# Eight PSUM accumulator tiles of one bank in place of two of four, in a decoder trunk on one core

## The chip, the core and the metric

The kernel runs on one core of one Trainium2 chip. The metric is the device time of one execution in microseconds (us), taken as the median of several runs. A profile is one further execution under the hardware profiler. The engines are named as in the profile: PE is TensorE's matmuls, PEld its weight loads, DVE is VectorE, ACT is ScalarE, SP issues the DMAs. L361 is line 361 of the kernel before.

## What is computed

Two layers over one sequence of 256 tokens and 2048 channels, in float32: a recurrent layer and an attention layer, each followed by a gated FFN with 5632 hidden channels.

```python
x = recurrent_block(x, norm1_g[0], lru_w_in, conv, gates, lru_lambda, lru_w_out)
x = swiglu_ffn(x, norm2_g[0], ffn_w_in[0], ffn_w_out[0])
k, v = shared_kv(x, kv_norm_g, w_kv, k_norm_g)
x = attn_block(x, norm1_g[1], w_q, q_norm_g, sinks, w_o, k, v)   # 32 heads of 64, window 128
x = swiglu_ffn(x, norm2_g[1], ffn_w_in[1], ffn_w_out[1])
...
def swiglu_ffn(x, g, w_in, w_out):
    gate, up = jnp.split(rms_norm(x, g) @ w_in, 2, axis=-1)
    return x + (jax.nn.silu(gate) * up) @ w_out
```

## The kernel before

**Jobs.** The work is a list of jobs, one for each weight tile of 128 x 1024 numbers (512 KB). `stream` (L335) goes through it: it loads the tile four jobs ahead, splits it three jobs ahead, and then issues the job's matmuls. A split (L306) makes of a float32 tile a rounded part `hi` on ScalarE (L314) and the rest `lo` on VectorE (L315). There are four buffers of each, so a split waits until PE has used the tile four jobs before. A product of two float32 matrices is three matmuls of such parts: hi by hi, hi by lo, and lo by hi.

**Groups.** Jobs come in groups that add up in four banks of PSUM (`group`, L365). A bank holds 512 float32 columns per partition, and there are eight. When the last job of a group is issued, `done` issues the operations that read its banks: `pull` (L398) or `residual` (L479, which adds into the residual stream `x`). The last job goes through the banks one after the other (L383), the earlier ones mix them. In some jobs (`SYNC`) a matmul is 512 columns wide and leaves two halves in a bank; then ScalarE copies one half to a temporary `t`, and VectorE adds the other.

**Banks.** `banks` is a queue of the eight banks: `bank` (L218) takes the first, `free_bank` puts one back at the end once its readers are issued, and `bank4` (L221) takes the four of one half of PSUM together, where all four are free. So a group has the four banks that were not in use by the group before it. Small products (norm statistics, transposes, scores, probabilities times values) take single banks with `mbank` (L240). In the kernel before, PSUM is two tiles, `b0` and `b1`, of four banks each, and a bank is a slice of one.

**Stages.** First the recurrent layer (`lru`): groups for four parts of the x branch and four of the y branch, and between them eight short gate jobs (`gates`, L839: 24 matmuls at L850 into four banks, each read by a sigmoid at L856), in the order x0 x1 x2 g0 x3 g1 y0 g2 g3 y1 g4 g5 y2 g6 g7 y3; then four groups of the output projection. Next an FFN with 22 groups into the hidden width and 4 out of it. Then keys and values, queries (L1235, two banks a group) with attention woven between, the output projection of attention (four groups), and the second FFN.

**Attention.** For each of 16 pairs of heads, `head_pair` issues: scores on PE (L1086), a masked sum and maximum on VectorE (L1097, which leaves the maximum in `h`), exponentials on ScalarE (L121), the division by their sum on VectorE (L139), transposes on PE (L1131), copies of these to SBUF on ScalarE (L121), the product with the values on PE (L1150), and a split of the result. The queries come to it through `finish`: splits of the query banks and transposes on PE (L1209).

**The product groups.** Groups 5, 7, ..., 17 of each FFN (`FAST`, seven per FFN) save matmuls: in six of their eight jobs seven products of 128 x 128 by 128 x 256 blocks stand for eight (`fast`, L541), and in the other two all eight are made (`plain`, L519). They add up in eight places of 256 columns, place h in bank h // 2 (`put`, L513). `joined` (L690) then sums the places into the gate and the up part, `at(h)` being place h. `fast` jobs write all places; the last job is `plain` and writes places 0 to 3 only, that is the two lower banks. A later job of the next group issues the transposes of the result (`turn`, L710, matmuls at L714).

**Order.** Each engine takes its instructions in order. The order in which the Python code issues them is set by half ticks of the job list (`half_tick`, `run_bg`), which let background tasks run as far as a count of VectorE and ScalarE time allows. The framework that builds the program then places each engine's instructions anew by what they depend on, and puts in the waits. All operations that go through `a`, `tt`, `stt`, `ts` have the lines L121, L130, L134, L139/L141.

## Time and profile before

| | us |
|---|---|
| median of 3 runs | 2086.24 (2085.16 to 2087.63) |
| profiled execution | 2089.25 |
| its span | 2087.5 |
| PE busy | 2013.3 (96%) |
| DVE busy | 1458.2 (70%) |
| ACT busy | 1125.1 (54%) |
| mean granted clock of PE | 0.989 |

The span is the time from the first to the last instruction of the profiled execution; the execution's own time lies a little above it. Busy times are shares of that span. A row of waits names who waited, for whose result, the time in total, how often, and the longest. In a row of the timeline the brackets at the end say how long the engine was idle before, and what ended that. PEclk is the clock that PE was granted, as a share of full speed.

### The profile page before, as it was taken

The numbers are of one execution on the slowest core, as the hardware profiler recorded it, in microseconds if no ns is written. First come the engines' busy times: TensorE is split into PE (matmuls) and PEld (weight loads), VectorE is DVE, ScalarE is ACT, GpSimd is POOL, SyncE is SP. The second block draws the span as 40 slices with busy tenths as digits, with TensorE's granted clock in tenths as the row PEclk, the third lists the DMA queues.
The fourth block names the chain that finished last, engine by engine and source line by source line (L and its number), as shares of the span: only waits on it lengthen the run. The fifth ranks groups of instructions, "written<-read, shape, count | busy, mean of one in ns | idle before, by whom it ended". The sixth has DMA issues, their size and how long they took to land. (4 is left out here: it accounts for less than half of the span.)

```text
span 2087.5 us, 39923 instructions
## 1 busy us (share of the span) xinstructions
PE 2013.3 (96%) x16487; PEld 1955.6 (94%) x16487; DVE 1458.2 (70%) x2291; ACT 1125.1 (54%) x1629; POOL 0.2 (0%) x4
## 2 busy tenths in 40 slices
PE   9999999999999999999998777999999999999999
PEld 9998999999999999999976567999999999999999
DVE  8878767888888955555576555677888889544443
ACT  7678755555555644444456555455555556444332
POOL 0000000000000000000000000000000000000000
PEclk9999999999999999999999999999999999999999
DMA  7545555555566655655652222545655565656663
GB/s 256 173 150 182 172 172 194 197 196 198 190 199 205 193 197 195 195 194 185 202 166 97 91 81 77 181 167 192 202 193 195 196 207 190 201 193 204 204 205 125
DMA packets 105016, 376.56 MB, mean 180 GB/s; under 512 B 11649, under 2 KB 13825, under 8 KB 104833
## 3 DMA queue, kind: packets, MB, share of 16 engines
q1 hardware_dynamic: 104544, 373.60, 54.1%
q8 instruction: 129, 2.11, 0.4%
q10 hardware_dynamic: 288, 0.40, 0.1%
q14 instruction: 55, 0.44, 0.1%
HBM read 371.86 MB, written 2.10 MB: 179 GB/s over the span
## 5 line engine op out<-in xcount | busy, mean ns | idle before, releaser
L361 PE MATMUL b<-s,hi 128*128 128x256 f32 (+1 forms) x8455 | 1138.6, 282 | 22.2 <-ACT s L121 8.5
L361 PEld LDWEIGHTS b<-s,hi 128*128 128x128 f32 x8455 | 1059.4, 189 | 38.2 <-ACT s L121 13.2
L315 DVE TENSOR_TENSOR lo<-raw,hi 128x1024 fp32r<-128x1024 f32 (+1 forms) x621 | 755.0, 1220 | 466.2 <-ACT hi L314 463.3
L314 ACT ACTIVATE hi<-raw 128x1024 fp32r<-128x1024 f32 (+1 forms) x621 | 653.4, 1056 | 636.0 <-PE b L361 497.9
L361 PE MATMUL b<-s,lo 128*128 128x256 f32 x4352 | 652.3, 278 | 0.9 <-DVE h L1097 0.9
L361 PEld LDWEIGHTS b<-s,lo 128*128 128x128 f32 x4352 | 568.9, 189 | 1.3 <-DVE h L1097 1.1
L328 ACT ACTIVATE s<-s 128x1024 fp32r<-128x1024 f32 x84 | 89.2, 1062 | 144.4 <-DVE s L327 143.6
L515 PE MATMUL b<-hi,s 128*128 128x256 f32 (+1 forms) x868 | 162.9, 291 | 0.0
L515 PEld LDWEIGHTS b<-hi,s 128*128 128x128 f32 x868 | 130.4, 189 | 3.8
L515 PE MATMUL b<-s,s 128*128 128x256 f32 x1008 | 133.3, 281 | 0.0
L515 PEld LDWEIGHTS b<-s,s 128*128 128x128 f32 x1008 | 125.2, 189 | 0.0
L330 DVE TENSOR_TENSOR s<-s,s 128x1024 fp32r<-128x1024 f32 x84 | 102.6, 1222 | 23.0 <-ACT s L328 22.3
L515 PE MATMUL b<-lo,s 128*128 128x256 f32 (+1 forms) x434 | 114.1, 289 | 0.0
L1235 PE MATMUL b<-hi,s 128*128 128x512 f32 x256 | 88.6, 427 | 14.3 <-ACT s L121 8.4
L121 ACT ACTIVATE s<-s 128x512 fp32r<-128x512 f32 (+3 forms) x172 | 82.9, 519 | 34.5 <-DVE s L130 25.1
L130 DVE TENSOR_TENSOR s<-s,s 128x512 fp32r<-128x512 f32 (+2 forms) x143 | 74.4, 549 | 12.1 <-ACT s L121 12.1
L121 ACT ACTIVATE s<-b 128x384 f32<-128x384 f32 (+4 forms) x112 | 51.1, 481 | 57.7 <-PE b L1235 10.8
L329 DVE TENSOR_TENSOR lo<-raw,hi 128x768 fp32r<-128x768 f32 x84 | 79.3, 950 | 0.0
L515 PEld LDWEIGHTS b<-lo,s 128*128 128x128 f32 x434 | 76.4, 188 | 1.8
L324 ACT ACTIVATE hi<-raw 128x768 fp32r<-128x768 f32 x84 | 70.2, 840 | 10.3 <-ACT hi L324 3.1
L1235 PEld LDWEIGHTS b<-hi,s 128*128 128x128 f32 x256 | 47.9, 199 | 27.7 <-ACT s L121 12.2
L325 DVE TENSOR_TENSOR s<-raw 128x512 f32<-128x512 f32 x84 | 57.6, 686 | 10.7 <-DMA raw<-in_ffn_in 10.6
(117 smaller groups left out, 1112.8 us busy)
## 6 DMA issues: line engine op xcount, KB each, us to landing
raw<-in_ffn_in SPq DMA_DIRECT2D x352, 512.0 KB, 3.4
raw<-in_ffn_out SPq DMA_DIRECT2D x176, 512.0 KB, 4.1
raw<-in_lru_in SPq DMA_DIRECT2D x63, 512.0 KB, 3.4
raw<-in_lru_out SPq DMA_DIRECT2D x32, 512.0 KB, 3.3
raw<-in_w_q SPq DMA_DIRECT2D x32, 512.0 KB, 3.3
raw<-in_w_o SPq DMA_DIRECT2D x32, 512.0 KB, 3.3
raw<-in_gate SPq DMA_DIRECT2D x8, 512.0 KB, 3.8
raw<-in_kv SPq DMA_DIRECT2D x8, 512.0 KB, 4.2
```

The costliest lines, as they stand in the source:

```text
L121: self.nc.scalar.activation(out, in_, func, **kw)
L130: self.nc.vector.tensor_tensor(out, a, b, op)
L314: self.nc.scalar.activation(hi[:, q], raw[:, q], AF.Copy)
L315: self.nc.vector.tensor_tensor(lo[:, q], raw[:, q], hi[:, q].bitcast(F32), ALU.subtract)
L324: act(hi[:, q], raw[:, q], AF.Copy)
L325: tt(two(d[:, 0:2 * T]), two(raw[:, T:3 * T]), raw[:, 0:T].unsqueeze(1).to_broadcast([P, 2, T]), ALU.subtract)
L328: act(mh[:, :], d[:, :], AF.Copy)
L329: tt(lo[:, q], raw[:, q], hi[:, q].bitcast(F32), ALU.subtract)
L330: tt(ml[:, :], d[:, :], mh[:, :].bitcast(F32), ALU.subtract)
L361: self.nc.tensor.matmul(ps[f][:, 0:c1 - c0], w, x2[k][:, c0:c1], start=f not in begun, stop=last and all(q[1] != f for q in todo[n + 1:]))
L515: nc.tensor.matmul(st["ps"][0][:, h * T:(h + n) * T], x, w, start=b not in st["begun"], stop=True, skip_group_check=True)
L1235: nc.tensor.matmul(st[g][b][:, :], x, q, start=c + kt == 0 and x is xh and q is wh, stop=c == 7 and kt == 1 and q is wl)
```

## The change

PSUM becomes eight tiles of one bank, `b0` to `b7`. The queue of banks, `bank4` and every matmul's place are as before: each matmul writes the same columns of the same physical bank. Since an instruction that reads two banks would now read two tiles, `joined` reads each with a sum of its own: the sum over places 3 and 4 and that over places 1 and 2 become two sums each, and those that need only the upper two banks come first.

```diff
-        self.sets = []
-        for i in range(2):
-            b = psum.tile([P, 2048], F32, name=f"b{i}")
-            self.sets.append([b, [b[:, 512 * j:512 * j + 512] for j in range(4)]])
-        self.banks = deque(b for q in self.sets for b in q[1])
+        self.sets = [[psum.tile([P, 512], F32, name=f"b{4 * i + j}") for j in range(4)] for i in range(2)]
+        self.banks = deque(b for q in self.sets for b in q)
...
         def put(h, x, w, n=1):
             b = h // 2
-            nc.tensor.matmul(st["ps"][0][:, h * T:(h + n) * T], x, w, start=b not in st["begun"], stop=True,
+            nc.tensor.matmul(st["ps"][b][:, h % 2 * T:(h % 2 + n) * T], x, w, start=b not in st["begun"], stop=True,
...
             def joined(q, g=g):
-                ps, banks = q
                 p1, c, u, h = self.half(), self.double(F32), self.slot(F32), self.slot(F32)
-                b = two(c[:, :])
                 twice = lambda ap: ap.unsqueeze(1).to_broadcast([P, 2, T])
-                at = lambda i, n=1: ps[:, i * T:(i + n) * T]
+                at = lambda i, n=1: q[i // 2][:, i % 2 * T:(i % 2 + n) * T]
                 self.a(p1, at(5))
-                self.tt(b[:, 0:4:3, :], two(at(3, 2)), twice(p1), ALU.add)
+                self.tt(c[:, 3 * T:4 * T], at(4), p1, ALU.add)
                 self.tt(two(u), two(at(6, 2)), twice(c[:, 3 * T:4 * T]), ALU.add)
                 self.tt(c[:, 3 * T:4 * T], at(7), u[:, 0:T], ALU.add)
-                self.tt(c[:, T:3 * T], at(1, 2), u, ALU.add)
+                self.tt(c[:, 0:T], at(3), p1, ALU.add)
+                self.tt(c[:, T:2 * T], at(1), u[:, 0:T], ALU.add)
+                self.tt(c[:, 2 * T:3 * T], at(2), u[:, T:2 * T], ALU.add)
                 self.tt(c[:, 3 * T:4 * T], at(0), c[:, 3 * T:4 * T], ALU.add)
-                for p in banks:
+                for p in q:
```

The rest of the diff fits `bank4` and `group` to the new lists. Lines after the first hunk are three lower in the changed kernel: its L358, L847, L1232, L127, L312 are L361, L850, L1235, L130, L315 of before. What the waits of the program are is seen in its order. In the rows below, a name is the tile written and those read, a number behind an underscore only keeps tiles apart, and the brackets name the engines whose counters an instruction waits for.

The first place is on PE in the recurrent stage, where the first gates (their last matmuls are in the first rows) are followed by the group x3. `b0_83` and `b1_84` are the halves of PSUM, `s0_140` is the input. Before:

```order
L850 MATMUL b0_83<-s14_771,lo0_79 128x256
L361 MATMUL b1_84<-s0_140,hi1_76 128x256 [waits Activation_49]
L361 MATMUL b1_84<-s0_140,hi1_76 128x256 x3
L361 MATMUL b0_83<-s0_140,hi1_76 128x256 [waits Activation_49]
L361 MATMUL b0_83<-s0_140,hi1_76 128x256 x11
```

The same place in the changed kernel, where `b2_85`, `b3_86`, `b4_87` and `b1_84` are the banks of the group and `b0_83` is the gates' last:

```order
L847 MATMUL b0_83<-s14_777,lo0_79 128x256
L358 MATMUL b2_85<-s0_146,hi1_76 128x256 [waits DVE_49,Activation_49]
L358 MATMUL b2_85<-s0_146,hi1_76 128x256
L358 MATMUL b3_86<-s0_146,hi1_76 128x256 [waits DVE_49]
L358 MATMUL b3_86<-s0_146,hi1_76 128x256
L358 MATMUL b4_87<-s0_146,hi1_76 128x256 [waits DVE_49]
L358 MATMUL b4_87<-s0_146,hi1_76 128x256
L358 MATMUL b1_84<-s0_146,hi1_76 128x256 [waits DVE_49]
```

The two waits for ScalarE before the first matmul of each half are now a wait for VectorE, which read this group's banks after x2, at each of the four banks, and one for the rounded weights (`hi1`).

The second place is on PE in attention, at the first job of the last query group (`s12` is its input), right after a product with the values (the line that writes 64 partitions). Before:

```order
L1150 MATMUL b0_83<-s6_12325,s2_11280 64x128
L1235 MATMUL b1_84<-hi0_75,s12_11350 128x512 [waits DVE_49,Activation_49]
L1235 MATMUL b1_84<-hi0_75,s12_11350 128x512
L1235 MATMUL b1_84<-lo0_79,s12_11350 128x512
L1235 MATMUL b1_84<-hi0_75,s12_11350 128x512 x2
L1235 MATMUL b1_84<-lo0_79,s12_11350 128x512
L1131 MATMUL b1_84<-con_65,s6_12325 128x128 [waits DVE_49] x2
```

In the changed kernel:

```order
L1147 MATMUL b2_85<-s6_12345,s2_11300 64x128
L1232 MATMUL b5_88<-hi0_75,s12_11370 128x512 x2
L1232 MATMUL b5_88<-lo0_79,s12_11370 128x512
L1232 MATMUL b6_89<-hi0_75,s12_11370 128x512 x2
L1232 MATMUL b6_89<-lo0_79,s12_11370 128x512
L1232 MATMUL b5_88<-hi0_75,s12_11370 128x512 x2
```

The query group's first matmul waits for nobody any more, and the transposes of a head pair (`con`) that stood in the middle of this job have moved behind it.

The third place is on VectorE at the end of the first product group: the sums of `joined` (they write `s19`, `s4` and `s1`) among the splits of weights (`lo`). Before:

```order
L315 TENSOR_TENSOR lo2_81<-raw2_73,hi2_77 128x1024 [waits DMAHW2_49,PE_49,Activation_49]
L315 TENSOR_TENSOR lo3_82<-raw3_74,hi3_78 128x1024 [waits DMAHW3_49,PE_49,Activation_49]
L130 TENSOR_TENSOR s19_5057<-b1_84,h1_90 128x2x256 [waits Activation_49]
L130 TENSOR_TENSOR s4_4839<-b1_84,s19_5057 128x512 [waits DVE_49]
L315 TENSOR_TENSOR lo0_79<-raw0_71,hi0_75 128x1024 [waits DMAHW4_49,PE_49,Activation_49]
L130 TENSOR_TENSOR s19_5057<-b1_84,s4_4839 128x256 [waits DVE_49]
L130 TENSOR_TENSOR s19_5057<-b1_84,s4_4839 128x512
L130 TENSOR_TENSOR s19_5057<-b1_84,s19_5057 128x256 [waits DVE_49]
```

In the changed kernel:

```order
L312 TENSOR_TENSOR lo2_81<-raw2_73,hi2_77 128x1024 [waits DMAHW2_49,PE_49,Activation_49]
L127 TENSOR_TENSOR s19_5063<-b6_89,h1_96 128x256 [waits Activation_49]
L127 TENSOR_TENSOR s4_4845<-b7_90,s19_5063 128x512 [waits DVE_49]
L127 TENSOR_TENSOR s19_5063<-b7_90,s4_4845 128x256 [waits DVE_49]
L127 TENSOR_TENSOR s19_5063<-b5_88,h1_96 128x256 [waits PE_49]
L127 TENSOR_TENSOR s19_5063<-b5_88,s4_4845 128x256
L127 TENSOR_TENSOR s19_5063<-b4_87,s4_4845 128x256 [waits PE_49]
L127 TENSOR_TENSOR s19_5063<-b4_87,s19_5063 128x256 [waits DVE_49]
L312 TENSOR_TENSOR lo3_82<-raw3_74,hi3_78 128x1024 [waits DMAHW3_49,Activation_49]
```

The sums are seven in place of five, stand together ahead of the split `lo3` in place of behind it and around `lo0`, and wait for PE twice on their way, once for each lower bank. The whole program has the same matmuls on the same banks, 28 instructions more on VectorE, and three table loads fewer on ScalarE (31 for 34).

More of the change, by code (lines that the diff above doesn't have):

```diff
@@ L222, in bank4 @@
         for q in self.sets:
-            if all(any(b is c for c in self.banks) for b in q[1]):
-                for b in q[1]:
+            if all(any(b is c for c in self.banks) for b in q):
+                for b in q:
                     self.drop(b)
@@ L227, in bank4 @@
                 self.sets.append(q)
-                return q
-        return [None, [self.bank() for _ in range(4)]]
+                return list(q)
+        return [self.bank() for _ in range(4)]
     def drop(self, b):
@@ L372, in mm @@
                 if c == 0:
-                    st["ps"] = self.bank4()[1] if four else [self.bank() for _ in range(4)]
+                    st["ps"] = self.bank4() if four else [self.bank() for _ in range(4)]
                     st["begun"] = set()
```

## The prediction

> **What bounds the kernel now.** I read the page's first lines, then a table of windows by stage, then what PE waited for in each stage, then the order of time at single waits.

> ```profile
> span 2087.5 us, 39923 instructions
> PE 2013.3 (96%) x16487; PEld 1955.6 (94%) x16487; DVE 1458.2 (70%) x2291; ACT 1125.1 (54%) x1629; POOL 0.2 (0%) x4
> ```

> PE is the bound and is idle for 74 us in all. The windows say where (columns: stretch, its length, busy time of PE, PEld, DVE, ACT, POOL, granted clock, DMA). The stages are: recurrent products, their output projection, the first FFN, keys and values, attention, its output projection, the second FFN, and what follows the last matmul.

> ```profile
> 20.00:250.00 230.00, 213.21 (x1724) 209.02 (x1724) 190.63 (x360) 174.57 (x292) 0.00 (x0) 0.98 0.52 173
> 250.00:345.00 95.00, 93.79 (x762) 91.03 (x761) 60.56 (x89) 48.63 (x74) 0.00 (x0) 1.00 0.55 185
> 345.00:1050.00 705.00, 704.85 (x6036) 698.74 (x6035) 506.84 (x679) 366.89 (x458) 0.00 (x0) 1.00 0.59 195
> 1050.00:1080.00 30.00, 28.33 (x183) 25.12 (x183) 25.13 (x37) 15.59 (x24) 0.00 (x0) 1.00 0.55 180
> 1080.00:1292.00 212.00, 169.87 (x987) 136.71 (x986) 120.87 (x378) 114.66 (x282) 0.00 (x0) 0.93 0.27 90
> 1292.00:1385.00 93.00, 86.83 (x694) 84.44 (x693) 56.82 (x86) 46.90 (x71) 0.00 (x0) 0.98 0.49 164
> 1385.00:2082.95 697.95, 697.79 (x5982) 691.86 (x5980) 481.89 (x621) 342.75 (x402) 0.00 (x0) 1.00 0.59 193
> 2082.95:2087.50 4.55, 0.00 (x0) 0.00 (x0) 1.41 (x4) 0.00 (x0) 0.00 (x0) 0.82 0.35 115
> ```

> In the two FFN stages, where the edited sums stand, PE misses 0.15 us in 705 and 0.16 in 698: nothing can be won there. The idle time is 16.8 us in the recurrent stage (230.00 - 213.21), 2.9 in the two short stages, 42.1 in attention and 6.2 in its output projection. The clock is below full in just those stages.

> What PE waited for up to 1050 us (columns: who waited, for whom, us in total, times, longest):

> ```profile
> PE b L361 <- ACT s L121: 8.5, 5, 2.4
> PE b L850 <- ACT s L121: 4.3, 3, 1.7
> PE b L850 <- ACT t L121: 1.9, 1, 1.9
> PE b L361 <- DVE s L130: 1.8, 1, 1.8
> ```

> These are 16.5 of the 16.8 us, and none is a split of a weight (L314, L315). One of them in order of time:

> ```profile
> 83.00 0.28 PE L850 MATMUL b<-s,lo 128*128 128x256 f32 x1
> 83.16 1.28 ACT L121 ACT_TABLE_LOAD   x1
> 84.45 1.57 ACT L121 ACTIVATE s<-b,par 128x256 f32<-128x256 f32 x4
> 85.71 0.58 PE L361 MATMUL b<-s,hi 128*128 128x256 f32 x1 [2.43 <-ACT s L121]
> ```

> After a block of gates, ScalarE loads a table and reads the four gate banks (the sigmoids of L856). The next x group starts only when the third of four has been read. It uses none of these banks: it has the four of the x group before it, which the row below shows read out by VectorE at 81.44 (80.35 + 1.09), before the gates' last matmul.

> ```profile
> 80.35 1.09 DVE L130 TENSOR_TENSOR s<-b,rstd 128x256 f32<-128x256 f32 x3 [0.28 <-PE b L361]
> ```

> So PE waits for a reader of another bank in the same four-bank tile. The order of before says the same: L361 waits for ScalarE there, and in the changed order it waits only for the readers of its own banks and for its split.

> The same in attention (rows of 1050 to 1292 us whose releaser does not make what the waiting line reads):

> ```profile
> PE b L1235 <- ACT s L121: 8.4, 6, 2.5
> PE b L1131 <- ACT s L121: 6.6, 3, 4.1
> PE b L1235 <- DVE h L1097: 3.2, 3, 1.2
> PE b L361 <- DVE h L1097: 3.1, 2, 2.2
> PE b L1209 <- DVE h L1097: 2.4, 1, 2.4
> PE b L1235 <- DVE s L130: 2.2, 1, 2.2
> PE b L1150 <- DVE h L1097: 0.6, 1, 0.6
> ```

> L1235 reads normed input and weight splits, L1131 what L139 normalised: a score's reader (L1097) or a copy out of PSUM (L121) gives them nothing. These rows are 26.5 us. The other 15.6 of the 42.1 are lines that wait for what may be their own data, and I count them as staying. Some of the 6.6 is data in truth and some of the 15.6 is not; I set these against each other.

> **The change part by part.**

> *Eight tiles.* Recurrent stage: 16.5 us of waits go. What is late next are the splits. There DVE is busy 190.63 of 230 and ACT 174.57, and one stretch is close to ScalarE's limit:

> ```profile
> 150.00:200.00 50.00, 46.55 (x386) 45.65 (x386) 43.20 (x80) 45.90 (x84) 0.00 (x0) 1.00 0.52 169
> ```

> Of its 3.45 us of idle PE I give half back: 1.7. In the short stages I take 1.2 of 2.9. In the output projection of attention these two rows, the last residual's reads holding the next group's first matmul, are 4.9:

> ```profile
> PE b L361 <- DVE x L130: 3.2, 1, 3.2
> PE b L361 <- ACT t L121: 1.7, 2, 0.8
> ```

> In attention the 26.5 us are 1.66 for each of 16 head pairs. PE then reaches the transposes of a pair's probabilities (L1131) sooner, and these wait for real data:

> ```profile
> 1175.55 1.01 DVE L139 TENSOR_SCALAR s<-s,h 128x128 f32<-128x128 f32 x4
> 1177.05 0.27 PE L1131 MATMUL b<-con,s 128*128 128x128 f32 x1
> ```

> The first of four normalising operations ends near 1175.8 and the last at 1176.56, so the slack is between 1.2 and 0.5 us. Of 1.66 us per pair, between 0.46 and 1.16 come back. I take 0.6, nearer the low end, since the readers of a pair also stop waiting for each other across banks: 16 x 0.6 = 9.6.

> *The clock.* After long waits PE runs slowly (window just behind the wait at 85.71, the next one, and one behind the 3.2 us wait):

> ```profile
> 85.70:89.10 3.40, 3.39 (x16) 3.39 (x17) 3.32 (x8) 2.18 (x5) 0.00 (x0) 0.51 0.02 6
> 89.10:92.50 3.40, 3.40 (x31) 3.40 (x31) 2.16 (x5) 3.03 (x4) 0.00 (x0) 1.00 0.43 154
> 1369.10:1372.50 3.40, 3.40 (x18) 3.40 (x17) 1.81 (x5) 1.36 (x2) 0.00 (x0) 0.50 0.10 42
> ```

> 16 to 18 matmuls in place of 31: about 1.5 us lost each time. In the recurrent stage the clock of 0.98 is 4.6 us of 230, all after such waits: 4.6 more. In the output projection one window: 1.5. In attention 0.93 is 14.8 us, PE is busy 0.80 of the stage, so 11.9 count; its idle time falls from 42.1 to 25.2 (15.6 + 9.6), by 40%, so 4.7 come back. The clock's terms are 4.6 + 1.5 + 4.7 = 10.8 us.

> [...]

> *The end.* The last four residual sums start after the last matmul:

> ```profile
> 2082.66 0.28 PE L361 MATMUL b<-s,lo 128*128 128x256 f32 x1
> 2082.98 0.42 DVE L130 TENSOR_TENSOR x<-x,b 128x256 f32<-128x256 f32 x1 [9.47 <-PE b L361]
> ```

> Four take 1.41 (x4 in the last window). The last job finishes its banks one after another (L383), six matmuls apart, so three sums can move beside matmuls: 1.41 - 0.42 = 1.0 us.

> *The sums.*

> ```profile
> L130 DVE TENSOR_TENSOR s<-b,s 128x512 f32<-128x512 f32 x28 | 19.1, 684 | 0.4
> L130 DVE TENSOR_TENSOR s<-b,s 128x256 f32<-128x256 f32 x28 | 11.6, 414 | 0.0
> ```

> Per product group two sums of 512 columns go and four of 256 come: 4 x 414 - 2 x 684 = 288 ns more on VectorE, 4.0 us over 14 groups. VectorE is busy 72% of that stage (506.84 of 705), and nobody waits on the sums but the transposes three jobs later: 0. Without that cover it would be 4.0. Moving the three sums that need only the upper banks ahead of the last job gains 0, since PE has no wait there. In the new order the sums stand ahead of a split (lo3) that is used three jobs on; that split's buffer is held by the group's last job anyway, so I cost the move at nothing. By the two orders ScalarE has three table loads fewer (31 for 34), of which I count nothing.

> **Sum.** 16.5 + 4.6 - 1.7 = 19.4 (recurrent); 1.2; 26.5 - 9.6 + 4.7 = 21.6 (attention); 4.9 + 1.5 = 6.4; 1.0. Together 49.6 us. The profiled execution took 2089.25 (span 2087.5 and 1.75 around it) and would take 2039.6; it lies 3.0 above the median of the runs, 2086.24, which becomes 2036.6, so 2037.

> **The rivals.**

> *All of it stays won.* Nothing gives back the 9.6 and the 1.7, and with the idle time down by 26.5 of 42.1 the clock returns 7.5 in place of 4.7: 49.6 + 9.6 + 1.7 + 2.8 = 63.7, so 2023. For it: every reader in attention waits less too. Against it: the slack of 0.5 to 1.2 us. Chance 0.16.

> *Attention is bound by the head pairs' own chain.* Every wait removed there reappears at L1131, L1150 and L1086, where 15.6 us wait for data already. Then 49.6 - 21.6 = 28.0 remain: 2058. For it: DVE and ACT are idle over 40% of that stage and PE waits all the same. Against it: the projection matmuls between are filler that needs no chain. Chance 0.17.

> *The clock does not follow these waits.* PE's slow windows come by another measure of its idleness and stay: 49.6 - 10.8 = 38.8, so 2047. The windows at 85.70 and 1369.10, each right behind a wait, speak against it. [...] Chance 0.04.

> *The change doesn't do what it says.* Two engines might hold each other up although their banks differ, and PE waits as before: 2086. [...] Chance 0.01.

> *Slower: readers ahead of splits.* The reads of a group's banks now stand earlier in the queues of VectorE and ScalarE, which take their work in order, and block there until PE has finished a bank. A split behind them comes late. It decides once a split is held longer than its lead, three jobs. Then each of 52 FFN groups (44 into the hidden width, 8 out) costs PE one split of VectorE:

> ```profile
> L315 DVE TENSOR_TENSOR lo<-raw,hi 128x1024 fp32r<-128x1024 f32 x619 | 753.6, 1222 | 462.3 <-ACT hi L314 459.4 <-ACT s L121 1.1
> ACT hi L314 <- PE b L361: 497.9, 325, 2.8
> ```

> 52 x 1.22 = 63 less 49.6: 2100. Against it: ScalarE waited 325 times for PE to release a split's buffer, so splits run as far ahead as their buffers let them. Chance 0.02.

> **How the numbers follow.** The forecast has 0.60, and its own bounds lie between the two nearest rivals. The range runs from the full gain with the 3.0 us of the short stages and of the output projection that I left out (2020) to the chain-bound attention with another 1.7 given back in the recurrent stage (2060). A measurement of this kernel tells a change of about 0.2%, 4 us, from none. Forecast and first three rivals are faster: 0.97; the fourth is within 0.2%: 0.01; the last is slower: 0.02.

> **What would show it.** Right: L361, L850 and L1235 have no waits on L121, L1097 or L130 reads; the recurrent stage has under 3 us of idle PE and a clock of 1.00; attention keeps 20 to 30 us of idle time, now at L1131, L1150 and L1086; one sum follows the last matmul; the FFN stages keep their length. Wrong: PE waits on L314 or L315 in the recurrent stage (splits too late), idle time of 40 us in attention, or an FFN stage longer by more than 2 us.

## The result and the profile after

| | before | eight tiles |
| --- | --- | --- |
| median of the runs, us | 2085.7 | 1993.0 |
| range of the runs, us | 2082.9 to 2087.6 | 1990.3 to 1994.6 |
| ratio to before | 1 | 0.9555, 95% interval 0.9539 to 0.9572 |

The change makes the kernel 4.45% faster, by 93 us. The forecast was 2037 us with a range of 2020 to 2060: the sign was right, and the gain is nearly twice the forecast. A few executions took from a third longer to four times as long as the others (2880, 5724 and 8052 us), and the medians of this document leave these out. The first lines of the page after:

```profile
span 1992.4 us, 39949 instructions
PE 1982.9 (100%) x16487; PEld 1935.5 (97%) x16487; DVE 1458.5 (73%) x2319; ACT 1123.0 (56%) x1626; POOL 0.2 (0%) x4
```

The span is 95.1 us shorter. PE's idle time fell by 64.6 us, from 74.1 to 9.5 (1992.4 - 1982.9). But PE's *busy* time also fell, by 30.4 us, with the same 16487 matmuls; where that comes from is shown below. The windows of after are cut at the same count of matmuls as the stages of before, so that equal work is compared (stretch, its length, busy time of PE, PEld, DVE, ACT, POOL, granted clock, DMA):

```profile
19.97:225.43 205.46, 202.80 (x1724) 200.37 (x1723) 187.37 (x357) 167.68 (x287) 0.00 (x0) 1.00 0.57 190
225.43:317.05 91.62, 91.56 (x762) 89.66 (x761) 61.90 (x93) 49.26 (x75) 0.00 (x0) 1.00 0.61 199
317.05:1021.64 704.59, 704.59 (x6036) 698.69 (x6034) 511.94 (x697) 370.69 (x460) 0.00 (x0) 1.00 0.59 195
1021.64:1049.54 27.90, 27.90 (x184) 25.30 (x182) 22.70 (x32) 14.79 (x20) 0.00 (x0) 1.00 0.55 178
1049.54:1204.33 154.79, 152.40 (x986) 126.07 (x985) 116.97 (x377) 111.89 (x279) 0.00 (x0) 1.00 0.38 125
1204.33:1288.57 84.24, 84.18 (x693) 81.81 (x693) 56.67 (x88) 47.73 (x75) 0.00 (x0) 1.00 0.55 181
1288.57:1989.36 700.79, 700.79 (x5981) 694.95 (x5979) 486.31 (x637) 345.84 (x402) 0.00 (x0) 1.00 0.58 192
```

Line by line against the stages of before (which were 230.0, 95.0, 705.0, 30.1, 211.9, 93.1 and 697.8 long when they are cut at these same matmuls): the recurrent stage is 24.6 us shorter, the two short stages 5.6, attention 57.1, its output projection 8.8, the first FFN 0.4; the second FFN is 3.0 longer. What lies ahead of the first stage and behind the last gives 1.6, and the sum is 95.1. The clock is 1.00 in every stage. Most of the miss is in one row: attention had 42.1 us of idle PE, and of these 2.4 are left. This is the whole list of what PE still waits for (who, for whom, us, times, longest):

```profile
PE b L463 <- DVE acc L127: 1.7, 1, 1.7
PE b L1274 <- DVE zero L1271: 1.3, 1, 1.3
PE b L358 <- ACT s L118: 1.2, 2, 0.8
PE b L1128 <- DVE s L136: 0.8, 3, 0.3
PE b L1083 <- ACT s L118: 0.7, 1, 0.7
PE b L1147 <- ACT s L118: 0.3, 1, 0.3
```

With a tile for each bank, none of these can be a wait for a reader of another bank, as forecast. But the transposes, the scores and the products with the values (L1128, L1083, L1147), at which I expected 20 to 30 us of attention's idle time, wait 1.8 us in all.

### The profile page after: what moved, and what is told of

It reads as the page before. It is cut to its first block, busy times and chain, and to the rows that moved or that the text cites. A ratio compares the mean times of both kernels' runs of the same rounds, so it can differ in the third digit from the quotient of the medians.

```text
span 1992.4 us, 39949 instructions
## 1 busy us (share of the span) xinstructions
PE 1982.9 (100%) x16487; PEld 1935.5 (97%) x16487; DVE 1458.5 (73%) x2319; ACT 1123.0 (56%) x1626; POOL 0.2 (0%) x4
## 5 line engine op out<-in xcount | busy, mean ns | idle before, releaser
L358 PE MATMUL b<-s,hi 128*128 128x256 f32 (+1 forms) x8455 | 1128.5, 280 | 1.6 <-ACT s L118 1.2
L312 DVE TENSOR_TENSOR lo<-raw,hi 128x1024 fp32r<-128x1024 f32 (+1 forms) x621 | 755.9, 1220 | 435.7 <-ACT hi L311 421.2
L358 PEld LDWEIGHTS b<-s,hi 128*128 128x128 f32 x8455 | 1051.7, 188 | 14.2 <-ACT s L118 2.0
L358 PE MATMUL b<-s,lo 128*128 128x256 f32 x4352 | 647.1, 277 | 0.0
L358 PEld LDWEIGHTS b<-s,lo 128*128 128x128 f32 x4352 | 564.7, 188 | 0.1
L327 DVE TENSOR_TENSOR s<-s,s 128x1024 fp32r<-128x1024 f32 x84 | 102.7, 1222 | 20.1 <-ACT s L325 19.9
L1232 PE MATMUL b<-hi,s 128*128 128x512 f32 x256 | 84.0, 408 | 0.0
L127 DVE TENSOR_TENSOR s<-s,s 128x512 fp32r<-128x512 f32 (+2 forms) x143 | 74.0, 549 | 4.4 <-ACT s L118 4.4
L118 ACT ACTIVATE s<-b 128x256 fp32r<-128x256 f32 (+4 forms) x112 | 49.9, 480 | 25.9 <-PE b L1128 7.9
L1232 PEld LDWEIGHTS b<-hi,s 128*128 128x128 f32 x256 | 45.8, 189 | 9.6 <-issue 1.4
```

The costliest lines, as they stand in the source:

```text
L118: self.nc.scalar.activation(out, in_, func, **kw)
L127: self.nc.vector.tensor_tensor(out, a, b, op)
L312: self.nc.vector.tensor_tensor(lo[:, q], raw[:, q], hi[:, q].bitcast(F32), ALU.subtract)
L327: tt(ml[:, :], d[:, :], mh[:, :].bitcast(F32), ALU.subtract)
L358: self.nc.tensor.matmul(ps[f][:, 0:c1 - c0], w, x2[k][:, c0:c1], start=f not in begun, stop=last and all(q[1] != f for q in todo[n + 1:]))
L1232: nc.tensor.matmul(st[g][b][:, :], x, q, start=c + kt == 0 and x is xh and q is wh, stop=c == 7 and kt == 1 and q is wl)
```

## The experiments

Each time is the median of the runs, beside runs of the kernel before on the same chip (medians 2084.3 to 2087.5 us).

| run | us | ratio to before, 95% |
| --- | --- | --- |
| e1_sums_only: old tiles, split sums | 2088.1 | 1.001 (0.9997 to 1.0024) |
| e4_half: one old tile, four of one bank | 2032.7 | 0.9741 (0.9718 to 0.9764) |
| e3_pairs: four tiles of two banks | 2019.3 | 0.9677 (0.9658 to 0.9697) |
| e2_old_order: eight tiles, old order on every engine | 2037.8 | 0.9769 (0.9747 to 0.9790) |
| e6_old_pe: eight tiles, old order on PE | 2011.7 | 0.9644 (0.9610 to 0.9677) |
| e7_old_readers: eight tiles, old order on all but PE | 2013.5 | 0.9646 (0.9623 to 0.9669) |
| e12_new_late: eight tiles, new order from the first FFN on | 1996.2 | 0.9593 (0.9568 to 0.9618) |
| e8_more_runs: after, more runs of wide matmuls | 1993.8 | 0.9550 (0.9529 to 0.9571) |
| e9_stop_2: after, 41 stops of 0.86 us | 2051.0 | 0.9848 (0.9828 to 0.9868) |
| e10_stop_4: after, 41 stops of 1.60 us | 2083.9 | 0.9981 (0.9970 to 0.9992) |
| e11_stop_7: after, 41 stops of 2.70 us | 2180.1 | 1.0469 (1.0450 to 1.0487) |
| e13_stop_12: after, 41 longer stops | 2295.0 | 1.1018 (1.0995 to 1.1042) |

**The sums alone.** The split sums with the tiles of before.

```
-        self.sets = [[psum.tile([P, 512], F32, name=f"b{4 * i + j}") for j in range(4)] for i in range(2)]
+        w = 4
+        big = [psum.tile([P, 512 * w], F32, name=f"b{i}") for i in range(8 // w)]
+        one = [big[i // w][:, 512 * (i % w):512 * (i % w) + 512] for i in range(8)]
+        self.sets = [one[0:4], one[4:8]]
```

> The two tiles of four banks stay; only the joined sums of the seven-product groups become sums over one bank. Theory A (the tiles cost the time, by waits on readers of other banks): no change from before, 2086 us within 4. Rival S (the sums gain or lose by themselves): VectorE has 288 ns more in each of 14 groups, so up to 4 us slower, 2090; or the upper banks read earlier give part of the gain, 2080 or less.

2088.1 us: no change. Attention waits as before (the window at the same matmuls):

```profile
1079.18:1286.60 207.42, 164.54 (x986) 132.18 (x985) 120.74 (x377) 114.41 (x282) 0.00 (x0) 0.95 0.28 92
```

That is 42.9 us of idle PE, against 42.1. The stage is 4.5 us shorter, since PE lost less to half clock behind the same waits (0.95 here, 0.93 in before); what lets the clock differ is seen with the stops below. The sums neither gain nor cost; the prediction's zero for them holds, and so does its cover (VectorE's slack in the FFN).

**A dose of the tile.** The same lines with `w = 2` (four tiles of two banks), and one tile of four banks beside four of one:

```
+        big = psum.tile([P, 2048], F32, name="b0")
+        self.sets = [[big[:, 512 * j:512 * j + 512] for j in range(4)],
+                     [psum.tile([P, 512], F32, name=f"c{j}") for j in range(4)]]
```

> Four tiles of two banks, the rest as in the changed kernel. Theory A: a wait stays only where reader and writer share a pair of banks, 1 of the 3 other banks of a set, so about a third of the loss stays: 1993 + 31 = 2024 us, within 15. Theory B: a gain only if the order comes out like that of eight tiles; anything between 2000 and 2086.

> One set stays a tile of four banks, the other becomes four tiles. Theory A: half of the loss stays if both sets are used alike: 1993 + 46 = 2040 us, within 15; PE's waits on readers are at banks of the first set only. Rival (loss needs only one joined set, since each second group meets it and PE stops there): 2060 or more.

2019.3 and 2032.7 us: both within the ranges of Theory A, so the loss grows with the banks that share a tile. Theory B allowed 2019.3 as well, and in these two kernels waits and order both change, so they don't tell the two apart. With the half change the waits on readers stand mostly, though not only, at the tile of four, whose name is b (c names the four of one bank):

```profile
PE b L360 <- DVE x L129: 5.7, 5, 3.7
PE b L360 <- DVE h L1096: 2.7, 1, 2.7
PE c L360 <- DVE s L129: 2.2, 1, 2.2
```

**The waits without the new order.** The framework places each engine's instructions anew for the new tiles. So the change has two parts: waits go, and instructions move. This kernel has the first alone: a program with the old tiles is laid out first, only to read its order, and the instructions of the real one are chained in it on each engine (`build(4)` has four banks to a tile, `build(1)` one). Its order is that of e1_sums_only on every engine, instruction by instruction.

```
...
+            for i, j in order or ():
+                tc.add_manual_dep(traced[j], traced[i].name, mybir.DependencyInfo(
+                    mybir.DependencyClass.NoSync, mybir.DependencyReason.DATA), reason="held order")
+        return nc, traced
+
+    nc, traced = build(4)
+    at = {i.name: n for n, i in enumerate(traced)}
+    last, order = {}, []
+    for i in [i for b in nc.main_func.blocks for i in b.instructions]:
+        if i.name in at:
+            if i.engine in last:
+                order.append((last[i.engine], at[i.name]))
+            last[i.engine] = at[i.name]
+    nc, _ = build(1, order)
...
```

> Eight tiles of one bank, but each engine's instructions are held in the order that they have with two tiles of four and the split sums: only the waits differ. Theory A (the waits themselves cost the time, also those of the readers ahead of the transposes, so that attention's chain of a head pair becomes shorter by itself): nearly all of the gain stays, 1990 to 2005 us, PE idle under 20 us. Theory B (the new order lets other matmuls stand between the steps of a head pair, and without it the waits come back at the transposes): attention keeps the 25.2 us idle of the prediction and 7.2 us of clock, so 2020 to 2035.

2037.8 us. Theory A falls and Theory B holds, though the time lies 3 us above its range: without the new order about half of the gain is lost. The forecast of 2037 us was, without my seeing it, a forecast of this kernel. Its recurrent stage and its attention:

```profile
20.25:229.59 209.34, 203.14 (x1725) 200.39 (x1724) 185.66 (x355) 170.42 (x288) 0.00 (x0) 1.00 0.56 185
1058.34:1245.06 186.72, 162.78 (x986) 132.94 (x985) 118.58 (x378) 111.91 (x282) 0.00 (x0) 0.95 0.31 102
```

Attention keeps 23.9 us of idle PE, where the prediction had 25.2 (15.6 that stay and 9.6 that come back), and 15 of them stand at the transposes, the first of the places that the prediction named (L1130 here; L138 normalises the probabilities). The three largest rows of the stage:

```profile
PE b L1130 <- DVE s L138: 12.4, 7, 4.0
PE b L1208 <- DVE s L129: 3.9, 2, 2.5
PE b L1130 <- ACT s L120: 2.1, 1, 2.1
```

The longest of these in order of time:

```profile
1164.78 1.18 PE L1085 MATMUL b<-s,s 128*128 128x128 f32 x8
...
1168.30 1.23 DVE L314 TENSOR_TENSOR lo<-raw,hi 128x1024 fp32r<-128x1024 f32 x1 [1.38 <-ACT hi L313]
1169.44 0.41 DVE L1096 CUSTOM_DVE_ANT_0 s<-b,con,par 128x128 f32<-128x128 f32 x1
...
1171.13 1.06 ACT L313 ACTIVATE hi<-raw 128x1024 fp32r<-128x1024 f32 x1 [2.86 <-PE b L1234]
...
1172.18 0.39 ACT L120 ACTIVATE s<-s,h 128x128 f32<-128x128 f32 x1
...
1174.47 1.01 DVE L138 TENSOR_SCALAR s<-s,h 128x128 f32<-128x128 f32 x4
...
1175.27 1.12 PE L1130 MATMUL b<-con,s 128*128 128x128 f32 x4 [4.00 <-DVE s L138]
```

The scores (L1085) are in PSUM by 1166, and VectorE reads them at 1169.44, since the split of a weight tile (L314) stands ahead of the read in its queue and waits for ScalarE. Then ScalarE could take the exponentials (L120 at 1172.18), but ahead of them stands another split (L313 at 1171.13), which waits for PE to free the weight buffer. PE has run out of matmuls meanwhile and waits for the probabilities. None of these is a wait for a neighbouring bank: it is the order of three queues. The same head pair in the changed kernel:

```profile
1143.91 1.08 PE L1083 MATMUL b<-s,s 128*128 128x128 f32 x8
...
1144.76 0.41 DVE L1094 CUSTOM_DVE_ANT_0 s<-b,con,par 128x128 f32<-128x128 f32 x1
...
1150.11 1.01 DVE L136 TENSOR_SCALAR s<-s,h 128x128 f32<-128x128 f32 x4
...
1150.85 0.82 PE L1128 MATMUL b<-con,s 128*128 128x128 f32 x6
```

The read starts at 1144.76, as soon as the first scores are there; the probabilities are normalised 6.2 us after the scores' first matmul in place of 9.7, and the transposes wait for nothing. PE has 28 matmuls between the last score and the first transpose of this pair in both orders; over all 16 pairs it has 756 in the new order and 670 in the old one, and for the last pair 42 and 18 (counted in the traces).

The reverse, the new order with the old tiles, wasn't run, so what the order alone would bring is not shown.

**Whose order.** The same chain, put on PE alone, and on every engine but PE; the framework places the rest.

```
-        if i.name in at:
+        if i.name in at and i.engine == mybir.EngineType.PE:
```

> Eight tiles; only TensorE keeps the order that it has with two tiles of four, the other engines are scheduled anew for it. Theory B1 (the place of the matmuls between a head pair's scores and its transposes decides): nearly all of the run with every engine's old order stays, 2025 to 2042 us, with attention's idle time again at the transposes. Theory B2 (the order on VectorE and ScalarE decides, with steps of a pair ahead of other work): 1993 to 2008 us.

> Eight tiles; VectorE, ScalarE and SyncE keep the order that they have with two tiles of four, TensorE is scheduled anew. Theory B1: TensorE finds matmuls to put before the transposes: 1993 to 2010 us. Theory B2: the steps of a pair stand as late as before and the waits remain: 2025 to 2042 us.

2011.7 and 2013.5 us: neither theory, both in part. Each side's order loses about 20 us, and the two together 45. Attention in the one and in the other:

```profile
1050.75:1226.40 175.65, 159.01 (x987) 130.65 (x985) 119.33 (x379) 113.88 (x282) 0.00 (x0) 0.96 0.33 111
```

```profile
1059.20:1226.49 167.29, 155.93 (x986) 128.86 (x985) 118.70 (x378) 111.58 (x282) 0.00 (x0) 0.98 0.36 117
```

Idle PE of 16.6 and 11.4 us there, between the 2.4 of the new order and the 23.9 of the old. Both the matmuls between a pair's steps and the readers' place ahead of the splits are needed. In attention PE's old order costs 20.9 us and the readers' 12.5. The readers' old order also has a recurrent stage of 213.9 us, 8.5 longer than in the changed kernel, and a part of that is the chance described two headings below.

**Where the order counts.** The old order (`a`) up to the first FFN, the new one (`b`) behind it, cut where both have had the same instructions.

```
+        n = min(cut, key=lambda n: abs(n / len(a) - CUT))
+        q = a[:n] + b[n:]
+        order += zip(q, q[1:])
```

> Eight tiles; every engine holds the order of two tiles of four up to the first FFN and the changed kernel's order behind it, so that attention alone, with its neighbours, has the new order. Theory D (what the held order cost, 2040 less 1993, lies in attention): recurrent stage as with the old order (209 us), attention as in the changed kernel (155): 1996 to 2002 us. Rival (each stage has its part of it, or attention's gain needs what stands ahead): 2008 or more.

1996.2 us: Theory D holds. Attention and its neighbours have nearly all of the order's gain (attention's row has 2.4 us of idle PE and a clock of 1.00, as in the changed kernel), and need nothing of what stands ahead. The profiled execution took 2004.5 us, 8.3 above the median, and its recurrent stage came out otherwise than expected, 214.8 us where the same order took 209.3:

```profile
20.17:234.94 214.77, 208.86 (x1724) 206.02 (x1723) 185.68 (x355) 170.95 (x288) 0.00 (x0) 0.99 0.55 180
1059.69:1214.47 154.78, 152.36 (x986) 126.12 (x985) 117.01 (x377) 111.94 (x279) 0.00 (x0) 1.00 0.37 125
```

It has no more idle time (5.9 us against 6.2) but 5.7 us more of busy PE, with the same instructions in the same order. A single stretch of 3.4 us at half clock is 1.7 of them. The rest leads to the next question.

**What lies in PE's busy time.** By the starts in the trace, matmuls of 256 columns follow each other at one of two distances, about 113 or about 118 ns, and keep one of them for hundreds of matmuls. The second FFN of the changed kernel has one such stretch, and here are 80 us of it, then the same work in before and in the run of 41 stops of 0.86 us, whose second FFN is the same program as after:

```profile
1671.00:1751.00 80.00, 80.00 (x674) 79.65 (x673) 43.30 (x48) 35.56 (x43) 0.00 (x0) 1.00 0.58 191
```

```profile
1767.60:1847.60 80.00, 80.00 (x699) 79.63 (x699) 45.43 (x49) 36.90 (x45) 0.00 (x0) 1.00 0.60 198
```

```profile
1729.40:1809.40 80.00, 80.00 (x702) 79.74 (x700) 46.20 (x51) 37.05 (x45) 0.00 (x0) 1.00 0.59 197
```

674 matmuls in place of 699 to 702, at the same clock and with no idle time. The kernel lets three matmuls of 512 columns run in a row in some jobs (`SYNC`), and behind some of these the distance goes from 118 to 113 (in after at 1235, 1302 and 1756 us). So I tried more of them.

```
-    SYNC = (0, 2, 5)
+    SYNC = (0, 2, 5)
+    LONG = (0, 2, 5, 7, 9, 11, 13, 15, 17, 19)
...
-                    at = sync.index(c) if run else 0
+                    at = sync.index(c) % 3 if run else 0
...
-            self.group(lambda c, g=g: w[g, c], nk, xs, done, g == 3, () if out is not None and g == 3 else self.SYNC)
+            self.group(lambda c, g=g: w[g, c], nk, xs, done, g == 3, () if out is not None and g == 3 else self.LONG if nk == NH else self.SYNC)
```

> The changed kernel with more jobs whose first matmuls are three of 512 columns in a row: in the FFN's output groups at jobs 7, 9, ... 19 too. Theory P (a disturbance leaves the start-to-start time of matmuls at 118 ns in place of 113, and three of 512 columns in a row set it right): the second FFN's first output group, at 118 ns for 88 us in the changed kernel, falls back after 30 us, which saves 2 to 3 us: 1990.5. Rival (the 118 ns go with the data or the buffers): no change, 1993.

1993.8 us, and the slow stretch ends at 1754 us as in after (1756), where the next group begins. Theory P fails as I put it: such runs alone don't set the distance right. Nor does the rival hold: the rows above show the same program at both. The same instructions ran at either distance (674 and 702 matmuls in 80 us); what sets it stays open.

**What a wait of PE costs.** Stops in the first FFN of the changed kernel, where PE otherwise never waits; every engine's order is held as it is there. Four settings of zeros on GpSimd stand between two matmuls at 41 places; the other runs have two, seven and twelve.

```
+                for i, j in stops:
+                    m = [nc.gpsimd.memset(trunk.idle[:, :], 0.0).ins for _ in range(IDLE)]
+                    dep(m[0], traced[i], mybir.DependencyClass.Sync)
+                    dep(traced[j], m[-1], mybir.DependencyClass.Sync)
```

> The changed kernel, each engine's order held, with 41 stops in the first FFN: after a matmul GpSimd sets four times 128x256 zeros, and the next matmul waits for it. w is the wait that the trace shows at each. Theory C (a wait of 2 us or more costs itself and about 1.5 us of half clock; a shorter one only itself): 1993 + 41 w if w is under 1.9, 1993 + 41 (w + 1.5) if w is over 2.1. Rival (the clock goes by the share of idle time over a longer stretch, not by single waits): 41 w in any case, clock 1.00. Theory P adds up to 137 matmuls x 4.6 ns = 0.6 us for each stop, 26 us together, less what runs of three 512-column matmuls set right.

> As the run with four settings of zeros at each of 41 stops, with two: a wait of about 1.0 us in place of 1.6. By that run a stop costs its wait, 0.3 us for filling the pipeline again and about 0.33 us for slower matmuls behind it: 41 x 1.63 = 67, so 2060 us. Theory C and its rival say the same here: clock 1.00.

> As before it, with seven settings: a wait of about 2.5 us. Without a loss of clock 41 x 3.13 = 128, so 2121 us, clock 1.00 (rival). With about 1.5 us of half clock behind each stop (Theory C) another 61, so 2183 us, and clock about 0.94 over the first FFN.

> As before it, with twelve settings: a wait of about 4.0 us. Without a loss of clock 41 x 4.63 = 190, so 2183 us (rival). Theory C: half clock for 1.5 us more behind each, 2245 us. If the threshold lies between 2.5 and 4 us, only this run shows it.

The first FFN with two, four and seven settings:

```profile
314.65:1079.62 764.97, 729.57 (x6035) 715.27 (x6034) 515.38 (x697) 373.48 (x460) 25.53 (x82) 1.00 0.54 180
```

```profile
315.16:1111.60 796.44, 730.87 (x6035) 716.57 (x6034) 515.79 (x697) 373.21 (x460) 51.04 (x164) 1.00 0.52 173
```

```profile
315.74:1211.84 896.10, 785.52 (x6036) 770.39 (x6035) 516.84 (x697) 373.80 (x460) 89.30 (x287) 0.93 0.46 153
```

Without stops the stage takes 704.59 us. Idle PE is 35.4, 65.6 and 110.6 us: 0.86, 1.60 and 2.70 at each stop. But the stage is longer by 60.4, 91.9 and 191.5. What is left for each stop is 0.61, 0.64 and 1.97 us. So four settings took 25 us more than the 2058.6 that waits alone would make (1993 + 41 x 1.60), two settings came 9 us below the expected 2060, mostly since the wait was 0.86 us and not 1.0, and seven settings, at 2180.1, met Theory C's 2183. The first two show a cost of every wait that the profile counts as *busy*: about 3000 more matmuls of the stage (3953 and 3863 for 875) start 118 ns apart, 14 us or 0.34 per stop, and the remaining 0.26 and 0.31 lie at the two ends of the stop. The profile draws the last matmul ahead of it 0.28 us long, where matmuls in a row start 0.12 apart, so the gap that it shows begins 0.16 us late; and the first matmul behind it is followed after 0.22 us, 0.11 more than usual. The third shows the clock, 1.35 us more per stop. One of its stops in order of time, and the window of 3.4 us behind it:

```profile
511.52 1.94 PE L361 MATMUL b<-s,hi 128*128 128x256 f32 x9 [2.70 <-POOL idle L1356]
```

```profile
511.50:514.90 3.40, 3.38 (x17) 3.38 (x18) 0.00 (x0) 1.06 (x1) 0.00 (x0) 0.57 0.22 88
```

The same of the run with four settings:

```profile
453.88 0.50 PE L361 MATMUL b<-s,lo 128*128 128x256 f32 x2 [1.60 <-POOL idle L1356]
```

```profile
453.85:457.25 3.40, 3.37 (x28) 3.37 (x29) 2.72 (x4) 1.17 (x2) 0.00 (x0) 1.00 0.55 177
```

By the traces' records of the granted clock, a stretch at half speed follows none of 41 waits of 0.86 us, one of 41 of 1.60 (the one that was 1.92), and 34 of 41 of 2.70; 1.35 x 41 / 34 = 1.6 us for each that does. The mean granted clock of the three executions was 1.000, 0.999 and 0.972. Theory C holds, and in these runs the clock follows single waits.

```profile
553.70:557.10 3.40, 3.36 (x28) 3.36 (x29) 0.00 (x0) 0.78 (x1) 0.00 (x0) 1.00 0.62 199
```

In before, twelve steps had 1.86 to 3.28 us of idle PE between matmuls, and each was followed by half speed; no step at full speed with 1.77 or less was. In other stages the border is less sharp: 1.44 us in one step were enough in the recurrent stage of e12_new_late, and 1.79 were not in the run with seven settings. The twelve settings took 2295.0 us, more than either number (7.4 us for each stop). By the steps between the other three its wait is about 4.5 us (an estimate: 2.70 + 5 x 0.37), which leaves about 2.8 us beyond the wait; what these are was not measured.

## Why the prediction was right or wrong

Terms of the sum in us, against the stage with the old order (waits gone, nothing moved) and against the changed kernel:

| step | forecast | old order | changed kernel |
| --- | --- | --- | --- |
| recurrent stage | 19.4 | 20.7 | 24.6 |
| two short stages | 1.2 | 3.1 | 5.6 |
| attention | 21.6 | 25.2 | 57.1 |
| its output projection | 6.4 | 5.4 | 8.8 |
| FFN stages, sums | 0 | -1.4 | -2.6 |
| the end (and the start) | 1.0 | 1.4 | 1.6 |
| sum | 49.6 | 54.4 | 95.1 |

The two columns on the right are single profiled executions; that of the old order lies about 3 us below the median of its runs (2035.0 and 2037.8), so its sum is nearer to 50 by the medians (2.31% of 2086.2 is 48.2).

- **False waits of the recurrent stage, 16.5 - 1.7, and its clock, 4.6: right.** 2.7 us of idle PE are left (forecast: under 3), the clock is 1.00, and PE waits on no split. The stage gained 5 us more than forecast, in part for the reason under *busy time* below, and in part by chance: 564 of its matmuls start 118 ns apart, and 1262 did before (3 us).
- **Attention, "15.6 that stay" and "9.6 that come back": this step failed.** Both were read from the waits of before, as if its instructions stood where they stood. With that order their sum is right: 23.9 us of idle PE, 15 of them at the transposes. Luck has a part in it, since one wait was read wrongly: the longest of those at the transposes that I counted as false, 4.1 us, is still 4.0 us with eight tiles and the old order, and waits for the normalised probabilities (L1130 at 1175.27 above). Other waits that I counted as staying went instead: the products with the values waited 4.1 us for ScalarE in before (L1150) and 0.3 with the old order in the new tiles. But the framework orders the instructions by the same tiles, and in the new order the readers of a pair stand ahead of the splits and more matmuls stand between its steps. I had the new order at hand and looked in it only for the waits that go. The idle time of the stage fell by 39.7 us, and of the 31.9 us by which the stage is shorter than with the old order (186.7 - 154.8), 11.1 come with the readers' new order alone and 19.4 with PE's.
- **The rival "all of it stays won" (2023) had the right direction for a wrong reason.** It had the readers wait less across banks; with the waits gone and the order held, they didn't wait less by enough. No rival had the new order hiding what were true waits.
- **The rival "attention is bound by the head pairs' own chain" fell.** The matmuls of the projections cover the chain where the order lets them: 2.4 us of idle PE are left in the new order, and 23.9 with the old one.
- **The clock, 10.8: the mechanism right, the size too small.** It follows the waits, as the stops show (half clock behind none of 41 waits of 0.86 us and behind 34 of 41 of 2.70), so the rival in which it doesn't fell. Since nearly all of attention's waits went, all of the 11.9 us of half clock in it came back in place of 4.7. The records of the clock put it higher, at 14.8 us: half of PE's busy time in the half-speed steps. In e1_sums_only, with the same idle time, it is 9.0, so about 5 of the 57.1 us are the chance of the one profiled execution of before.
- **Busy time: a term that the sum lacked.** In the stops of 0.86 and 1.60 us a wait cost 0.26 and 0.31 us more than its gap in the trace, so about 0.28. Before has 51 waits of over 0.15 us, the changed kernel 8: 43 x 0.28 = 12 us, an estimate, as the 0.28 was measured in an FFN alone. With 64.6 us of idle time and 18 us of clock (4.6, 11.9 and 1.5) this makes 94.6 of the 95.1. So close a sum is luck: with the 21.6 us of the clock's records (5.1, 14.8 and 1.7) it is 98.2, and how the 30.4 us divide between clock and waits is not known to better than 3 or 4 us. PE was busy for 96% of the span of before, and 30.4 us of the loss lay inside this busy time. The matmuls at 118 ns cost about the same in both (3932 and 3725 of them in all: 1 us of difference).
- **The end, 1.0: right.** One sum stands behind the last matmul in place of four, and the time from the last matmul's end to the end of the span fell by 1.5 us:

```profile
1989.08 0.28 PE L358 MATMUL b<-s,lo 128*128 128x256 f32 x1
1989.40 0.42 DVE L127 TENSOR_TENSOR x<-x,b 128x256 f32<-128x256 f32 x1 [0.26 <-PE b L358]
```

- **The sums and the reads ahead of the splits, 0: right.** The first FFN is 0.4 us shorter. The second is 3.0 longer, which the prediction named as a sign against it; but PE has no idle time in it, VectorE and ScalarE don't hold it up, and the same program ran there without the loss (702 matmuls in 80 us). It is the chance of the two distances (1568 matmuls at 118 ns, and 848 before: 3.3 us), not a queue. So the slower rival, readers ahead of splits, fell: no PE wait stands at a split.
- **"The change doesn't do what it says": fell.** With a tile for each bank PE waits 6.0 us in all, in the list above, so no such hold-up shows here. Before, the waits were in effect by four banks, and that, order and waits together, is what the 4.45% were.

## What to carry to other kernels

Where a framework derives both the waits and the order from its tiles, a tile that joins independent buffers costs twice, and what a finer tile brings can't be read from the waits of the old trace alone: compare the two orders at each true wait that you count as staying. Hold the old order in the new program to tell the two parts apart. And price a wait of TensorE above the gap that the trace shows: here about 0.28 us each, and about 1.6 us more behind 34 of 41 waits of 2.7 us, according to how the wait fell on the clock's steps of 3.41 us.

## What the runs showed that I had not expected

- In these traces matmuls of 256 columns start about 113 or about 118 ns apart, for hundreds in a row, at a clock of 1.00 in both. The same instructions in the same order took 209.3 us in one run and 214.8 in another, with 554 and 1480 matmuls at the longer distance (926 x 4.6 ns = 4.3 us of the 5.4). A few us either way in a stage are therefore nothing to explain by an edit.
- Most stops of TensorE were followed by the longer distance: behind 37 of the 41 stops of 0.86 us, and of 1.60 us too, matmuls start 118 ns apart. About 3000 more of the stage's 6000 do, which is 0.34 us for each stop.
